# Row tails, router rows and the last attention denominators moved between engines in a two-layer mixture-of-experts backbone

## The chip, the cores and the metric

The kernel runs on one core of one Trainium2 chip. The metric is the device time of one execution in microseconds (us). The names of the engines are those of the profile: PE (matmuls), PEld (its weight loads), DVE (vector), ACT (scalar), POOL (GpSimd) and SP, which here only issues transfers. Each engine takes its instructions in order from a queue of its own, and semaphores make one engine wait for another.

## The reference, cut to what matters

512 latent and 256 context tokens of width 1024 pass through two post-norm layers. Layer 0 mixes with attention (8 neighbourhood heads and 8 grouped-query heads), layer 1 with two recurrences (RWKV-7 and mLSTM). After each mixer stand the output weight, a layer norm, a router that picks 6 of 64 experts for each token, the experts, one shared expert and a second layer norm. Layer 1 keeps the latent tokens alone.

```python
x = layer_norm(DN_ALPHA * x + g1 * (m_lat @ mix_w_out[i]), ln_g[i, 0], ln_b[i, 0])
h_lat = x * (1.0 + sc2) + sh2
...
scores = jax.nn.sigmoid((xt @ router_w).astype(F32))
_, idx = lax.top_k(scores + router_b.astype(F32), TOP_K)
gates = jnp.take_along_axis(scores, idx, -1)
...
y = yb.reshape(n_rows, D) * row_gate[:, None]
return jax.ops.segment_sum(y, row_tok, num_segments=n_tok + 1)[:n_tok]
...
x = layer_norm(DN_ALPHA * x + g2 * y[:B * S].reshape(B, S, D), ln_g[i, 1], ln_b[i, 1])
```

## The kernel before, in words

Tokens lie in tiles of 128 rows: six in layer 0 (four latent, two context), four in layer 1. A scheduler that simulates a timeline sets the order on each engine's queue, so moving one line of code can move others; what it chose is read from the order rows below. Stages of the profiled execution, in us from the start of the span:

- 0 to 485: layer 0's attention. A head pair (a "row" of `mT`) is closed by `close_block`: the reciprocal of the sums (L614, `rs`), the eviction of the unnormalized output, then three steps on POOL's queue: a transfer of `rs` to DRAM (L617), two transfers back that spread it over 64 partitions each (L620), and a multiply (L622). The last row is row 3.
- 485 to 640: the output weight. `weights` loads it in blocks and splits each into two parts, `w_hi` on ACT (L409) and `w_lo` on DVE (L410); `mT` is split in the same way, row by row; three matmuls (L414 to L416) make one product. The load buffer `w` shares a tag, and so memory, with `h2`. Then for each tile `first_norm` (L1087 to L1091: two DVE passes make `h`, one ACT and two POOL passes make the row `x` that the second norm needs) and `route` (L951 to L979: logits, the six best, `mask`, ranks and gates).
- 640 to 660: `sort` makes the list of each expert's tokens: gates in three parts (L932 to L936), one-hot rows `oh` (L1179), list matmuls (L1184); instructions L1363 to L1383 count what overflows the planned units.
- 660 to 1352: the routed experts of layer 0 in 49 units: a gather (L1207), transposes (L1258, L1260, L1261), up (L1217 into `pb`), gate, down (L1217 into `pp`), eviction of `py` to `y` in halves (L1247 on ACT, L1248 on DVE), and a scatter that adds to `acc` in DRAM (L1249).
- 1352 to 1404: the second norm's rows: the sums come back (L1410), then for each tile add, times g2 (L1415, L1416, halves on DVE and POOL), the residual (L1417), statistics (L878 to L882) and ACT's L1419.
- 1404 to 2161: the recurrent layer; it sends small state tiles through DRAM by SP (L2178 and L2181).
- 2161 to 2254: output weight, router and sort of layer 1; to 2861 its 37 units; to 2923 its end: the last scatters, L1410 to L1419 for four tiles, the final gain and offset (L2417 and L2418: DVE takes 640 columns, POOL 384), and the store.

The functions that the diff touches, with their line numbers:

Of the kernel before, what the change touches and what calls it, by code (L numbers as in the profile page):

```python
# [12 lines left out]
F32 = mybir.dt.float32  # L13
# [3 lines left out]
AF = mybir.ActivationFunctionType  # L17
# [338 lines left out]
class Kern:  # L356
# [152 lines left out]
    def attention(self, mT):  # L509
# [100 lines left out]
        def close_block(po, sums, out):  # L610
# [4 lines left out]
            self.copy(out, po)  # L615
            d = self.dr.tile([2 * n, 128], F32, name="rsum", tag=f"rsum{n}", bufs=2)
# [7 lines left out]
        def outputs(g, b, pTs, v, cols, state, sums, row):  # L624
# [5 lines left out]
            if b == 3:  # L630
                close_block(state[g], sums[:, 0:4], mT[:, row, 0:NLAT])
            if b == 5:
                close_block(state[g], sums[:, 4:6], mT[:, row, NLAT:])
# [253 lines left out]
    def layer_tail(self, layer, mT, x_rows, finish, part=None, done=None):  # L887
# [7 lines left out]
        with ExitStack() as es:  # L895
# [34 lines left out]
            def gates(dst, src, rest):  # L930
# [5 lines left out]
                nc.vector.tensor_copy(dst[:, :, :, 5], rest)  # L936
# [86 lines left out]
            with ExitStack() as es2:  # L1023
# [5 lines left out]
                def weights(b, parts=None):  # L1029
# [52 lines left out]
                def first_norm(t):  # L1082
# [13 lines left out]
                if layer == 0:  # L1096
                    room = Room(ring.tile([128, 2048], F32, name="sw1"),
# [25 lines left out]
                sw += [third(i["shared_w"][layer, k], ring, f"sw{k}") for k in range(len(sw), 3)]  # L1123
# [11 lines left out]
            def sort():  # L1135
# [33 lines left out]
                gates(aux, pq[:, :, 1], gq)  # L1169
# [68 lines left out]
            def down(hT, parts, ws, idx):  # L1238
# [8 lines left out]
                nc.scalar.copy(y[:, 0:512], py[:, 0:512])  # L1247
                nc.vector.tensor_copy(y[:, 512:], py[:, 512:])  # L1248
# [4 lines left out]
            def columns_of(xg):  # L1253
# [3 lines left out]
                for k in range(KT):  # L1257
                    nc.tensor.transpose(p[:, k], xg[:, k * 128:(k + 1) * 128], self.k_ident[:n, :n])  # L1258
                out = wp.tile([128, KT, 128], F32, name="xT", tag="xT", bufs=2)[:, :, :n]
                nc.scalar.copy(out[:, 0:4], p[:, 0:4])  # L1260
                nc.vector.tensor_copy(out[:, 4:8], p[:, 4:8])  # L1261
# [94 lines left out]
            for _ in side:  # L1356
                pass
# [1082 lines left out]
```

## Time and profile before

| | us |
|---|---|
| median of 3 runs | 2927.14 (2916.27 to 2935.19) |
| the profiled execution | 2924.99 |
| its span, first to last instruction | 2923.0 |

| engine | busy us | share of the span |
|---|---|---|
| PE | 2418.9 | 83% |
| DVE | 1214.3 | 42% |
| POOL | 760.8 | 26% |
| ACT | 737.1 | 25% |

The granted TensorE clock is 0.898 of full speed over the span, and the transfers move 247 GB/s in the mean. The shares are averages over stages with different limits: what one stage waits for is read from that stage's own rows.

### The profile page before, as it was taken

What the parts mean: (1) busy time and instruction counts of PE and PEld (TensorE: products, weight loads), DVE (VectorE), ACT (ScalarE), POOL (GpSimd) and SP (SyncE); (2) the same over time, 40 slices, a digit from 0 to 9 for tenths busy, and PEclk for the clock granted to TensorE, in tenths of its full rate; (3) what the DMA queues carried; (4) which work ended last, traced back from release to release, by engine and by line L of the source; (5) the groups of instructions that cost most, each with busy time, mean ns of one, the idle gap of its engine ahead of it and who ended that gap; (6) DMA issues with size and microseconds to landing.
All of it is one profiled execution on the core that took longest, in us unless ns stands there. A gap on an engine that the chain in (4) does not pass through costs nothing. (4 is left out here: it accounts for less than half of the span.)

```text
span 2923.0 us, 45988 instructions
## 1 busy us (share of the span) xinstructions
PE 2418.9 (83%) x18007; PEld 1469.8 (50%) x18007; DVE 1214.3 (42%) x2595; ACT 737.1 (25%) x1605; POOL 760.8 (26%) x674
## 2 busy tenths in 40 slices
PE   7789895969989999994799778866866988979981
PEld 6658664854434444331578666756755333324330
DVE  5742544473212222213753577856566212111114
ACT  3442443231101111111554443413222101111102
POOL 0111011121112222214344354434622111111114
PEclk9899997879999999997899787879976999999995
DMA  8644445658999999996224445589635999999993
GB/s 315 213 127 124 111 132 99 236 199 313 377 343 327 359 332 347 378 343 197 86 71 111 132 126 153 145 238 299 241 129 214 383 378 354 358 393 353 353 378 115
DMA packets 254089, 722.31 MB, mean 247 GB/s; under 512 B 111096, under 2 KB 137464, under 8 KB 194736
## 3 DMA queue, kind: packets, MB, share of 16 engines
q1 hardware_dynamic: 216656, 631.86, 59.2%
q0 software_dynamic: 26560, 68.09, 9.3%
q10 hardware_dynamic: 10656, 19.40, 2.1%
q8 instruction: 143, 2.34, 0.4%
q14 instruction: 74, 0.61, 0.1%
HBM read 636.45 MB, written 107.33 MB: 254 GB/s over the span
## 5 line engine op out<-in xcount | busy, mean ns | idle before, releaser
L1217 PE MATMUL pb<-ew,xT 128*32 128x512 f32 (+2 forms) x3504 | 658.6, 605 | 24.4 <-DMA ew<-in_moe_w_dram 15.4
L1217 PEld LDWEIGHTS pb<-ew,xT 128*32 128x32 f32 (+2 forms) x3504 | 210.5, 127 | 397.3 <-issue 353.9
L1217 PE MATMUL pp<-ew,hT 128*32 128x512 f32 (+2 forms) x1752 | 327.2, 603 | 7.7 <-DMA ew<-in_moe_w_dram 5.2
L1432 DVE SCALAR_TENSOR_TENSOR hs<-s,gate,pb 128x256 f32<-128x256 f32 x86 | 41.3, 480 | 649.7 <-ACT s L1427 633.9
L1207 POOL DMA_INDIRECT xg<-rows,idx x86 | 88.8, 1032 | 649.4 <-PE pp L1258 276.0
L1427 ACT ACTIVATE s<-pb 128x256 f32<-128x256 f32 x96 | 36.1, 383 | 769.9 <-PE pb L1217 746.7
L1249 POOL DMA_INDIRECT acc<-ye,idx x86 | 137.0, 1593 | 323.9 <-DMA acc<-ye,idx 146.8
L1217 PEld LDWEIGHTS pp<-ew,hT 128*32 128x32 f32 (+2 forms) x1752 | 101.6, 126 | 189.1 <-issue 175.0
L414 PE MATMUL pp<-h_hi,w_hi 128*128 128x512 f32 (+1 forms) x432 | 162.5, 377 | 8.7 <-DVE mT L389 4.3
L415 PE MATMUL pp<-h_lo,w_hi 128*128 128x512 f32 (+1 forms) x432 | 159.7, 370 | 1.0 <-DVE h_lo L410 1.0
L416 PE MATMUL pp<-h_hi,w_lo 128*128 128x512 f32 (+1 forms) x432 | 159.7, 371 | 0.5 <-POOL w_lo L1570 0.5
L1570 POOL TENSOR_TENSOR w_lo<-w,w_hi 128x512 fp32r<-128x512 f32 x66 | 91.6, 1388 | 148.3 <-ACT w_hi L1569 127.9
L1258 PEld LDWEIGHTS pp<-consts,xg 128*128 128x128 f32 x688 | 79.5, 146 | 70.5 <-issue 47.4
L1258 PE MATMUL pp<-consts,xg 128*128 128x128 f32 x688 | 98.3, 288 | 14.4 <-DVE sh L1311 6.8
L1248 DVE COPY ye<-pp 128x512 f32<-128x512 f32 x86 | 59.1, 687 | 114.7 <-ACT ye L1247 109.6
L414 PE MATMUL pb<-w_hi,m_hi 128*128 128x256 f32 x256 | 77.9, 308 | 26.6 <-ACT w_hi L409 16.2
L414 PEld LDWEIGHTS pp<-h_hi,w_hi 128*128 128x128 f32 x432 | 86.9, 202 | 24.6 <-issue 6.8
L416 PEld LDWEIGHTS pp<-h_hi,w_lo 128*128 128x128 f32 x432 | 87.0, 202 | 16.4 <-issue 3.4
L440 PE MATMUL pb<-ada_w,cz 128*32 128x256 f32 x640 | 54.1, 456 | 49.6 <-DMA ada_w<-in_ada_w_dram 49.5
L1261 DVE COPY xT<-pp 128x512 f32<-128x512 f32 x86 | 59.4, 690 | 84.9 <-ACT xT L1260 84.9
L415 PEld LDWEIGHTS pp<-h_lo,w_hi 128*128 128x128 f32 x432 | 87.3, 202 | 14.1 <-issue 2.3
L1247 ACT COPY ye<-pp 128x512 f32<-128x512 f32 x86 | 50.4, 588 | 166.3 <-PE pp L1217 110.0
(515 smaller groups left out, 4737.5 us busy)
## 6 DMA issues: line engine op xcount, KB each, us to landing
ew<-in_moe_w_dram SPq DMA_DIRECT2D x384, 1024.0 KB
ada_w<-in_ada_w_dram SPq DMA_DIRECT2D x48, 1024.0 KB
w<-in_rec_w_dram ACTq DMA_DIRECT2D x66, 256.0 KB
steps<-dL SPq DMA_DIRECT2D x16, 1024.0 KB
acc<-zero SPq DMA_DIRECT2D x12, 1024.0 KB
ew<-acc SPq DMA_DIRECT2D x10, 1024.0 KB
w<-in_att_w_dram SPq DMA_DIRECT2D x18, 512.0 KB
cells<-dM SPq DMA_DIRECT2D x8, 1056.0 KB
```

The source lines that it names most:

```text
L414: mm(out, l_hi, r_hi, start=start, stop=False)
L415: mm(out, l_hi, r_lo, start=False, stop=False)
L416: mm(out, l_lo, r_hi, start=False, stop=stop)
L440: nc.tensor.matmul(p[32 * g:32 * g + 32], self.cz[:, 4 * a + g, 30 - 2 * i:62 - 2 * i], w[:, 4 * a + g, :], start=i + a == 0, stop=i + 1 = ...
L1207: nc.gpsimd.indirect_dma_start(out=xg, out_offset=None, in_=self.rows[layer], in_offset=bass.IndirectOffsetOnAxis(ap=idx, axis=0), bounds_ ...
L1217: nc.tensor.matmul(out[s], x[:, s], ws[m], start=start, stop=stop, tile_position=(0, s.start))
L1247: nc.scalar.copy(y[:, 0:512], py[:, 0:512])
L1248: nc.vector.tensor_copy(y[:, 512:], py[:, 512:])
L1249: nc.gpsimd.indirect_dma_start(out=self.acc[layer], out_offset=bass.IndirectOffsetOnAxis(ap=idx, axis=0), in_=y, in_offset=None, bounds_ch ...
L1258: nc.tensor.transpose(p[:, k], xg[:, k * 128:(k + 1) * 128], self.k_ident[:n, :n])
L1261: nc.vector.tensor_copy(out[:, 4:8], p[:, 4:8])
L1570: nc.gpsimd.tensor_tensor(lo, w, hi.bitcast(F32), op=OP.subtract)
```

## The change

1. `close_block` has an argument `at_once`, true for row 3: the reciprocals stand on diagonals (DVE, new L623), a matmul with ones spreads them (PE, L624), and DVE multiplies (L626). The other rows keep POOL's way.
2. `first = loaded_part()`: the first load buffer of the output weight is allocated ahead of the other tiles.
3. Layer 0's first shared weight is loaded after the loop over tiles.
4. `first_norm`: ACT's pass and POOL's two become two DVE passes, new L1105 and L1106.
5. The overflow count is issued after the last `columns_of`; the gather for unit 2 waits for the sort and the first transposes.
6. In layer 1 the eviction multiplies by g2 (one DVE instruction of 1024 columns), and g2's row is loaded ahead of the first gathers.
7. `finish`, with the final gain's and offset's loads, is called ahead of the last `close`.
8. The second norm's rows are whole DVE instructions; in the last layer two of them take the place of L1419 and of the four half passes.

```diff
-        def close_block(po, sums, out):
+        def close_block(po, sums, out, at_once):
...
+            if at_once:
+                pr = self.bank((128, n * 128))
+                diag = ap.tile([128, 512], F32, name="r", tag="r", bufs=1)
+                for b in range(n):
+                    for s in range(2):
+                        d = diag[:, 256 * (b % 2) + 128 * s:][:, :128]
+                        nc.vector.tensor_scalar(d, self.k_ident, rs[:, s * n + b:s * n + b + 1], None, op0=OP.mult)
+                        nc.tensor.matmul(pr[s * 64:s * 64 + 64, b * 128:(b + 1) * 128], self.k_ones[:, 0:64], d,
+                                         start=True, stop=True, tile_position=(0, 64 * s))
+                nc.vector.tensor_tensor(out, out, pr, op=OP.mult)
+                return
...
-                close_block(state[g], sums[:, 0:4], mT[:, row, 0:NLAT])
+                close_block(state[g], sums[:, 0:4], mT[:, row, 0:NLAT], row == 3)
...
+                def loaded_part():
+                    return rp.tile([128, 4, 256], F32, name="w", tag="h2", bufs=2)
...
-                        w = rp.tile([128, 4, 256], F32, name="w", tag="h2", bufs=2)
+                        w = first if first is not None and k == 0 else loaded_part()
...
+                first = loaded_part()
...
-                w = [weights(0, w0)]
+                w = [weights(0, w0, first)]
...
-                    nc.scalar.activation(x, x, AF.Identity, bias=both, scale=over)
-                    nc.gpsimd.tensor_tensor(x, x, ra, op=OP.mult)
-                    nc.gpsimd.tensor_tensor(x, x, rbb, op=OP.add)
+                    nc.vector.scalar_tensor_tensor(x, x, less, ra, op0=OP.add, op1=OP.mult)
+                    nc.vector.scalar_tensor_tensor(x, x, over, rbb, op0=OP.mult, op1=OP.add)
...
-                sw = [third(i["shared_w"][layer, k], ring, f"sw{k}") for k in range(3 if layer else 1)]
+                sw = [third(i["shared_w"][layer, k], ring, f"sw{k}") for k in range(3 if layer else 0)]
...
+                if layer == 0:
+                    nc.sync.dma_start(sw0, i["shared_w"][layer, 0])
+                    sw = [sw0] + [third(i["shared_w"][layer, k], ring, f"sw{k}") for k in (1, 2)]
...
-                nc.scalar.copy(y[:, 0:512], py[:, 0:512])
-                nc.vector.tensor_copy(y[:, 512:], py[:, 512:])
+                if layer:
+                    nc.vector.tensor_tensor(y, py, g2[0], op=OP.mult)
+                else:
+                    nc.scalar.copy(y[:, 0:512], py[:, 0:512])
+                    nc.vector.tensor_copy(y[:, 512:], py[:, 512:])
...
+            if layer:
+                g2 = [self.row(wp, layer, "g20")]
...
-            sort()
+            sorted_ = sort()
             load()
-            xgs[2] = fetch(slot_of(2)[0])
             xT = columns_of(xgs.pop(0))
+            with tc.issue_after(columns_of.last.ins), tc.issue_after(sorted_.ins):
+                xgs[2] = fetch(slot_of(2)[0])
...
+            fresh = lambda: wp.tile([128, 2048], F32, name="ew", tag="ew", bufs=RING)
+            done = finish(fresh)
             close(len(units) - 1)
...
+            late = ExitStack()
+            late.enter_context(tc.issue_after(columns_of.done.ins))
...
-                for eng, c in zip((nc.vector, nc.gpsimd), half):
-                    eng.tensor_tensor(y[:, c], y[:, c], more[:, c], op=OP.add)
-                    eng.tensor_tensor(y[:, c], y[:, c], g2[st[t]][:, c], op=OP.mult)
+                nc.vector.tensor_tensor(y, y, more, op=OP.add)
+                if not layer:
+                    nc.vector.tensor_tensor(y, y, g2[st[t]], op=OP.mult)
                 nc.vector.scalar_tensor_tensor(x, y, 1.0, x, op0=OP.mult, op1=OP.add, accum_out=sums[:, t:t + 1])
-                less, over, both = self.spread(wp, x, sums[:, t:t + 1], y)
-                nc.scalar.activation(x, x, AF.Identity, bias=both, scale=over)
-                done(t, x)
+                done(t, x, *self.spread(wp, x, sums[:, t:t + 1], y))
...
-                for eng, c in ((nc.vector, slice(0, 640)), (nc.gpsimd, slice(640, D))):
-                    eng.tensor_tensor(x[:, c], x[:, c], gain[:, c], op=OP.mult)
-                    eng.tensor_tensor(x[:, c], x[:, c], offset[:, c], op=OP.add)
+                nc.vector.scalar_tensor_tensor(x, x, less, gain, op0=OP.add, op1=OP.mult)
+                nc.vector.scalar_tensor_tensor(x, x, over, offset, op0=OP.mult, op1=OP.add)
```

DVE's queue at the last heads and the split of `mT`, before (L614 is the reciprocal of the last sums, L389 copies out of PSUM):

```order
L614 RECIPROCAL rs<-sums_3889 128x2x2
L389 COPY pT<-pb 128x256 x2
L389 COPY mT<-pb 128x256
L1047 MEMSET sums 128x24
L410 TENSOR_TENSOR m_lo<-mT,m_hi 128x768 x7
L410 TENSOR_TENSOR w_lo<-w,w_hi 128x1024 x2
L943 CAST upper<-consts 128x128
```

and with the change:

```order
L615 RECIPROCAL rs<-sums_3889 128x2x2
L623 TENSOR_SCALAR r<-consts,rs 128x128
L389 COPY pT<-pb 128x256
L626 TENSOR_TENSOR mT<-mT,pb 128x512
L623 TENSOR_SCALAR r<-consts,rs 128x128 x4
L389 COPY mT<-pb 128x256
...
L626 TENSOR_TENSOR mT<-mT,pb 128x256
L410 TENSOR_TENSOR m_lo<-mT,m_hi 128x768
```

The multiply now stands on DVE right behind the eviction, and all eight `m_lo` stand ahead of both `w_lo`; before, seven stood there and the eighth behind POOL's multiply.

DVE's queue in layer 0's sort, before (L1363 to L1383 are the overflow count, L932 to L936 the gates):

```order
L1383 CAST blk<-ov 1x1
L932 CAST aux<-pp 128x384
L1179 TENSOR_TENSOR oh<-slot,rk 128x768
...
L1371 TENSOR_REDUCE oc<-ov 128x1
L933 TENSOR_TENSOR ye<-pp,aux 128x384
```

and with the change, where they are L944 to L948 and `oh` is L1197:

```order
L944 CAST aux<-pp 128x384
L945 TENSOR_TENSOR ye<-pp,aux 128x384
L946 CAST aux<-ye 128x384
L947 TENSOR_TENSOR ye<-ye,aux 128x384
L948 CAST aux<-ye 128x384
L1197 TENSOR_TENSOR oh<-slot,rk 128x768
```

The count has left this place, and the gates stand together ahead of the one-hots. On PE the first eight transposes (L1258, now L1279) stand ahead of the list matmuls instead of behind them.

SP's queue in the recurrent layer, before (state tiles to DRAM and back):

```order
L2030 DMA dL_11595<-Arb_15989 128x2x256
L2178 DMA dT_13241<-Tb_15976 64x16x16 x4
L2030 DMA dL_11595<-TT_15860 128x2x256
L1884 DMA cells_16424<-in_mlstm_order_dram 128x256
L2181 DMA T0_13238<-dT_13241 64x8x64 x8
```

and with the change, though no line of that layer is edited:

```order
L2054 DMA dL_11595<-Arb_15989 128x2x256
L2202 DMA dT_13241<-Tb_15976 64x16x16 x2
L1925 DMA cells_16423<-dR_11600 128x1024
L2205 DMA T0_13238<-dT_13241 64x8x64
L2202 DMA dT_13241<-Tb_15976 64x16x16
L2205 DMA T0_13238<-dT_13241 64x8x64
```

Writes and reads of the same state now alternate here; before, four writes stood together ahead of eight reads.

## Rows read from the trace of the kernel before

**Rows 1.** Windows: stretch, its us, PE busy (instructions), granted clock, DMA share, GB/s.
```profile
485.00:516.00 31.00, 9.84 (x42) 0.56 0.94 197
562.00:640.00 78.00, 57.90 (x440) 0.82 0.41 153
2254.00:2400.00 146.00, 129.88 (x939) 0.96 1.00 391
```

**Rows 2.** Timeline of PE: start, us, engine, line, operation, [idle before <-releaser].
```profile
495.70 1.01 PE L414 MATMUL pb<-w_hi,m_hi 128*128 128x256 f32 x3 [10.75 <-ACT w_hi L409]
...
511.80 0.58 PE L414 MATMUL pb<-w_hi,m_hi 128*128 128x256 f32 x1 [10.21 <-ACT m_hi L409]
```

**Rows 3.** Timeline of POOL and of SP, the same stretch.
```profile
510.17 0.71 POOL L622 TENSOR_TENSOR mT<-mT,r 128x256 f32<-128x256 f32 x1 [3.03 <-DMA r<-rsum]
484.99 0.80 SPq L1033 DMA_DIRECT2D w<-in_w_out_dram  x2
```

**Rows 4.** Timeline of DVE, the same stretch.
```profile
486.21 5.29 DVE L410 TENSOR_TENSOR m_lo<-mT,m_hi 128x768 fp32r<-128x768 f32 x6
491.44 1.23 DVE L410 TENSOR_TENSOR w_lo<-w,w_hi 128x1024 fp32r<-128x1024 f32 x1
...
497.23 0.22 DVE L946 TENSOR_SCALAR slot<-consts 128x128 bf16<-128x128 f32 x1
```

**Rows 5.** Groups of DVE by form, 560 to 660: form, count, busy us, mean ns, idle.
```profile
L969 DVE CAST mask<-m 128x128 bf16<-128x128 f32 x6 | 7.8, 1306 | 0.2
...
L1088 DVE SCALAR_TENSOR_TENSOR h<-h,rstd,B 128x1024 f32<-128x1024 f32 x6 | 7.7, 1278 | 0.0
L968 DVE TENSOR_TENSOR m<-rep,bi 128x64 f32<-128x64 f32 x6 | 6.4, 1074 | 0.2
```

**Rows 6.** Timelines of DVE and POOL in one router tile.
```profile
588.61 0.23 DVE L962 TENSOR_TENSOR bi<-sc,bias 128x64 f32<-128x64 f32 x1
...
594.60 2.38 DVE L969 CAST mask<-m 128x128 bf16<-128x128 f32 x1
...
594.56 2.34 POOL L1091 TENSOR_TENSOR x<-x,rb 128x1024 f32<-128x1024 f32 x1
```

**Rows 7.** Timeline of PE in the two sorts, layer 0 then layer 1.
```profile
658.65 0.58 PE L1184 MATMUL pb<-aux,oh 128*128 128x6 bf16 x30 [7.84 <-DVE aux L936]
...
2250.37 0.38 PE L1184 MATMUL pb<-aux,oh 128*32 128x6 bf16 x32 [5.90 <-DVE oc L1374]
2250.68 3.27 PE L1258 MATMUL pp<-consts,xg 128*128 128x128 f32 x16
```

**Rows 8.** What DVE's half eviction L1248 waited for, 2254 to 2861: us, times.
```profile
  ACT ye L1247: 39.1, 13
```

**Rows 9.** Groups of DVE by form, 1360 to 1405, second norm of layer 0.
```profile
L1417 DVE SCALAR_TENSOR_TENSOR x<-ew,x 128x1024 f32<-128x1024 f32 x6 | 10.1, 1688 | 1.5 <-POOL ew L1416 1.2
L1415 DVE TENSOR_TENSOR ew<-ew 128x512 f32<-128x512 f32 x6 | 7.2, 1200 | 15.6 <-DMA ew<-acc 15.6
L1416 DVE TENSOR_TENSOR ew<-ew,g 128x512 f32<-128x512 f32 x6 | 7.0, 1161 | 0.1
L882 DVE TENSOR_TENSOR rstd<-rstd 128x1 f32<-128x1 f32 x6 | 3.0, 506 | 0.1
```

**Rows 10.** Timelines of SP and DVE: sums fetched and first used, layer 0 then 1.
```profile
1363.89 3.30 SPq L1410 DMA_DIRECT2D ew<-acc  x6
...
1368.99 0.69 DVE L1415 TENSOR_TENSOR ew<-ew 128x512 f32<-128x512 f32 x1 [15.58 <-DMA ew<-acc]
...
2878.18 2.37 SPq L1410 DMA_DIRECT2D ew<-acc  x4
...
2885.72 0.69 DVE L1415 TENSOR_TENSOR ew<-ew 128x512 f32<-128x512 f32 x1 [18.73 <-DMA ew<-acc]
```

**Rows 11.** Timeline of POOL, its last row, at the end.
```profile
2916.85 1.45 POOL L2418 TENSOR_TENSOR x<-x,ew 128x384 f32<-128x384 f32 x1
```

**Rows 12.** Waits of PE in the recurrent layer: us in total, times, longest.
```profile
PE pb L394 <- DMA T<-dT: 13.1, 2, 8.4
```

More of the change, by code (lines that the diff above doesn't have):

```diff
@@ L630, in outputs @@
             if b == 3:
-                close_block(state[g], sums[:, 0:4], mT[:, row, 0:NLAT])
+                close_block(state[g], sums[:, 0:4], mT[:, row, 0:NLAT], row == 3)
             if b == 5:
-                close_block(state[g], sums[:, 4:6], mT[:, row, NLAT:])
+                close_block(state[g], sums[:, 4:6], mT[:, row, NLAT:], row == 3)
         def run_blocks(items, first, second, third, lag):
@@ L1027, in layer_tail, with weights @@
                 w_parts = lambda: [rp.tile([128, mk, 256], F32R, name=v, tag=v, bufs=wb) for v in ("w_hi", "w_lo")]
-                def weights(b, parts=None):
+                def loaded_part():
+                    return rp.tile([128, 4, 256], F32, name="w", tag="h2", bufs=2)
+                def weights(b, parts=None, first=None):
                     hi, lo = parts or w_parts()
                     for k in range(0, mk, 4):
-                        w = rp.tile([128, 4, 256], F32, name="w", tag="h2", bufs=2)
+                        w = first if first is not None and k == 0 else loaded_part()
                         self.loads = nc.sync.dma_start(w, i["w_out"][layer, b, :, k:k + 4])
@@ L1122, in layer_tail @@
                     pass
-                sw += [third(i["shared_w"][layer, k], ring, f"sw{k}") for k in range(len(sw), 3)]
+                if layer == 0:
+                    nc.sync.dma_start(sw0, i["shared_w"][layer, 0])
+                    sw = [sw0] + [third(i["shared_w"][layer, k], ring, f"sw{k}") for k in (1, 2)]
                 route(rp, turn[-1], hs.pop(turn[-1]))
@@ L1168, in sort @@
                 nc.scalar.copy(rk, pq[:, :, 0])
-                gates(aux, pq[:, :, 1], gq)
+                return gates(aux, pq[:, :, 1], gq)
             def slots(members, at):
@@ L1257, in columns_of @@
                 for k in range(KT):
-                    nc.tensor.transpose(p[:, k], xg[:, k * 128:(k + 1) * 128], self.k_ident[:n, :n])
+                    columns_of.last = nc.tensor.transpose(p[:, k], xg[:, k * 128:(k + 1) * 128], self.k_ident[:n, :n])
                 out = wp.tile([128, KT, 128], F32, name="xT", tag="xT", bufs=2)[:, :, :n]
                 nc.scalar.copy(out[:, 0:4], p[:, 0:4])
-                nc.vector.tensor_copy(out[:, 4:8], p[:, 4:8])
+                columns_of.done = nc.vector.tensor_copy(out[:, 4:8], p[:, 4:8])
                 return out
@@ L1349, in layer_tail @@
                     slot_of(n + LISTS)
-                if n == 6:
+                if n == 6 and not layer:
                     with tc.issue_after(self.loads.ins):
@@ L1383, in layer_tail @@
             nc.vector.tensor_copy(blk[:, 128:129], cum[0:1, NE - 1:NE])
+            late.close()
             n_more = nc.values_load(blk[0:1, 128:129], min_val=0, max_val=127)
@@ L1400, in layer_tail @@
                 down(gated(up(xT, all_of, [w[0:2]]), gate[:, 0:1]), all_of, [w[2]], idx[:, 1])
-            fresh = lambda: wp.tile([128, 2048], F32, name="ew", tag="ew", bufs=RING)
-            done = finish(fresh)
             sums = wp.tile([128, nt], F32, name="sums")
-            half = slice(0, 512), slice(512, D)
             ys = {}
@@ L2388, in keep, with rows @@
         def keep(room):
-            def rows(t, x):
+            def rows(t, x, less, over, both):
+                nc.scalar.activation(x, x, AF.Identity, bias=both, scale=over)
                 if t < 4:
@@ L2413, in store, with rows @@
             gain, offset = (k.row(None, 1, v, out=w[:, n * D:n * D + D]) for n, v in enumerate(("fg", "fb")))
-            def rows(t, x):
-                for eng, c in ((nc.vector, slice(0, 640)), (nc.gpsimd, slice(640, D))):
-                    eng.tensor_tensor(x[:, c], x[:, c], gain[:, c], op=OP.mult)
-                    eng.tensor_tensor(x[:, c], x[:, c], offset[:, c], op=OP.add)
+            def rows(t, x, less, over, both):
+                nc.vector.scalar_tensor_tensor(x, x, less, gain, op0=OP.add, op1=OP.mult)
+                nc.vector.scalar_tensor_tensor(x, x, over, offset, op0=OP.mult, op1=OP.add)
                 nc.sync.dma_start(out[0, t * 128:(t + 1) * 128], x)
```

3 lines of the change are left out of this document (2 added, 1 removed).

## The prediction

> **What bounds the kernel now.** I read the windows by stage first, then PE's timeline for its idle stretches, then, for what ended each, the timelines and the groups by form of the engine named. PE is busy 83% of the span, so a saving counts only where PE, or the end of the program, waits for it. The reader should see four kinds of stretch. Between the attention and the output weight PE works 9.84 of 31 us [rows 1]: it waits 10.75 us for ACT's `w_hi` and then 10.21 us for ACT's last `m_hi` [rows 2]. In layer 0's router PE is busy 57.9 of 78 us [rows 1]. The experts of layer 1 are bound by transfers: DMA share 1.00 [rows 1]. In the second norms PE has nothing to do, and DVE and POOL set the length.
>
> **The change, part by part.** The sum is made against the profiled execution, 2924.99 us; the median of the three runs, 2927.14, is 2.15 above it.
>
> *Attention to output weight (edits 1 to 3).* Before, the last denominators go through DRAM; the last multiply starts at 510.17, having waited 3.03 us for the spread rows [rows 3]. Then ACT casts, and PE starts at 511.80 [rows 2]. The two weight loads are issued only at 484.99 [rows 3], when the last attention matmuls have freed the memory of their buffer. With the change both loads can be issued during the attention, and eight diagonals (price: the 128x128 tensor-scalar, 0.22 [rows 4], so 1.8 us) lie on a DVE that then waits for PE. I follow DVE's new queue: the last multiply ends at about 486; small casts and fills some 3.5 us; eight `m_lo` at 5.29/6 = 0.88 each, 7.1; two `w_lo` at 1.23, 2.5 [rows 4]. That ends at about 499. In the trace of before both `w_lo` and the eighth `m_lo` were done, and PE ran without gaps, from about 512 on. PE has about 5 us of the first products to do in either case and can do them while DVE still splits. 512 - 499 is 13; I take **12** because ACT now casts eight `m_hi` ahead of the first `w_hi`. Bounds: 8 (only the second wait goes) and 14. The first shared weight hides behind the tiles: it is first used with the experts, after 640; without that cover its 1 MB costs 2.7 us, at the 391 GB/s of [rows 1].
>
> *Router rows (edit 4).* What goes is not POOL's time but what it does to DVE. A 64-column tensor-tensor takes 0.23 us on DVE alone; the mask's cast takes 2.38 when it starts within POOL's 2.34 us multiply-add [rows 6]. Over six tiles the mean is 1.306 for that cast and 1.074 for L968 [rows 5]; against 0.23 that is 1.08 + 0.84 = 1.9 us a tile, and three more small forms lose about 1.1 between them, so about 3.1 in all. Added are two passes of 1.28 (L1088's mean [rows 5]), 2.56, in front of the same mask. Net 0.5 a tile: **3** for six tiles in layer 0, 2 for four in layer 1. Bounds: 0 (the first of the two new passes also waits for ACT's square) and 9 in layer 0, if the idle stretches of the matmuls close.
>
> *Sorts (edit 5).* The list matmuls waited 7.84 us in layer 0 and 5.90 us in layer 1, there for `oc` of the overflow count [rows 7]. The count leaves, worth about 1 us of instructions between the gates (estimate from the order: eight instructions of the 64-column kind, partly behind ACT); and eight of the 16 transposes that follow in 3.27 us [rows 7] move into the wait, 1.6. I take **2.5** for each, between 1 and 5. The gather for unit 2 now waits for the sort; it is needed two units later (692 us for 49 units, so 28 us). The count itself ends up in DVE's idle time between the last units.
>
> *Layer 1 in transfers.* Its router and sort give 2 + 2.5; but the stage behind is bound by loads, which start with the router's end and not with the sort's. I count **3.5** (0 to 5). Edit 6 costs nothing there: DVE's half eviction already waited for ACT's (39.1 us in 13 cases [rows 8]), so one instruction ends about when two in a row did. g2's row is the same 0.5 MB, moved.
>
> The Trainium skill speaks against that edit: PSUM — Partial Sum Buffer, "Specifications (TRN2)", says that ScalarE and VectorE read PSUM in parallel at full bandwidth when they are on different banks. By it the halves cost 0.69 us together and one DVE instruction about 0.5 more, 37 times 18 us; the trace disagrees, for the halves ran one behind the other.
>
> *Second norm of layer 0 (edit 8).* DVE's rows for six tiles sum to 10.1 + 7.2 + 7.0 + 3.0 = 27.3 us [rows 9]. New: two whole tensor-tensors at 1.23, one pass at 1.28, 0.15 for L882: 3.9 a tile, 23.3. With the wait of 1.2 for POOL [rows 9] gone it is 5; DVE's queue also carries the reciprocal's wait for ACT, so I take **4** (2 to 6).
>
> *The end (edits 7 and 8).* In layer 0 DVE starts 5.1 us after the first issue of L1410, in layer 1 7.5 us after [rows 10]. The two rows ahead of it, 1 MB, are now loaded earlier, and SP's 0.86 us for them too: first sum at 2877.3 + 5.1 = 2882.4 instead of 2885.7. A tile then costs DVE 1.23 + 3 x 1.28 + 0.4 = 5.5 us, four tiles 22, and about 2 us of waits for ACT's squares at the first and last tile: 2906.4. Before, POOL's last row ended at 2918.3 [rows 11]. The store behind it stays. That is **12** (7 to 14).
>
> Sum: 12 + 3 + 2.5 + 3.5 + 4 + 12 = 37, so 2924.99 - 37 = **2888 us**. All lower bounds together are 18 (2907), all upper ones 53 (2872).
>
> **The rivals.**
>
> *The recurrent layer's new order takes it back.* No line of it is edited, but its queues are (SP's rows with `dT`). PE waits there 8.4 us at most for such a read [rows 12]. Writes and reads now alternate, so a read that waits for its write to land holds SP's next write. Against: many of these reads are not waited for (2 waits in all, 13.1 us). Two more waits make 2905, a chance of 0.17. **The slower side** is the same mechanism repeated: above five such waits (37 / 8.4 = 4.4) the kernel is slower than before, and with eight, 8 x 8.4 = 67, it takes 2955. Chance 0.06.
>
> *DVE becomes the bound.* If the slow small forms wait for something other than POOL, nothing comes back for the 2.56 us a tile: instead of 3 and 2 gained, 15 and 10 lost in front of `route`, part of it hidden behind PE's matmuls of the next tile; half of it on the path gives 2888 + 5 + 12 = 2905. For it: DVE has more to do in every stage touched. Against: start and end of the cast and of POOL's row coincide [rows 6]. Chance 0.10.
>
> *The clock comes back too.* From 485 to 516 the granted clock is 0.56, in the router 0.82 [rows 1], that is 1.2 GHz for part of the time, behind the idle stretches. If these close, up to 0.18 of 78 us is run at 2.4 GHz where it was 1.2, and half of that was bound by PE: 7 us more, and by likeness as much in layer 1's router, so 2874. Against: the stretches there are cut, not closed. Chance 0.07. The Trainium skill (TensorE: Matmul & The Clock Gate, "What's actually happening") states the rule behind it, that activity releases the throttle; the trace agrees in the clock of those stretches.
>
> *The change doesn't do what it says.* If the buffers moved ahead meet another tile's memory, the loads still wait for the attention and only the second wait goes: 2892, inside the forecast's range.
>
> **How the numbers follow.** Forecast 0.60 (2872 to 2907), clock 0.07, order with two more waits 0.17, DVE 0.10, slower 0.06. The range is 2868 to 2913: below it lies a share of the clock's case, above it the slower case and the tails of the two at 2905. A measurement of this kernel tells about 1% from no change: 2898 and 2956. Under 2898: five sixths of the forecast, the clock, a sixth of the two at 2905, 0.50 + 0.07 + 0.05 = 0.62. Slower by over 1%: half of the slower case, 0.03. Within 1%: 0.35.
>
> **What would show it.** PE's 10.75 and 10.21 us gone, with the matmuls of the output weight dense from about 499. The mask's cast near 0.25 in every tile. PE's waits in the sorts at 5 and 4 us. The first sum at the end about 5 us after its issue, DVE's 1024-column passes at 1.2 to 1.3, and the last one about 12 us ahead of POOL's 2918.3, less what came before. The recurrent layer as long as before, 757 us, within 8. It is wrong if that layer lengthens by more, or if whole-row passes cost 2 us with POOL silent.

## The result and the profile after

| | before | changed |
|---|---|---|
| median of 4 runs, us | 2921.7 (2915.5 to 2935.19) | 2875.44 (2870.79 to 2889.01) |
| the profiled execution, us | 2924.99 | 2889.01 |
| its span, us | 2923.0 | 2887.2 |
| granted clock | 0.898 | 0.900 |
| busy DVE / POOL / ACT, us | 1214.3 / 760.8 / 737.1 | 1214.1 / 661.6 / 705.5 |

The changed kernel takes 0.983 of the time before (95% interval 0.980 to 0.986), 1.7% less; the forecast was 2888 in 2868 to 2913. The medians lie 46 us apart, the two spans 35.8: the profiled execution of the changed kernel is the slowest of its four. What follows goes by the spans, and by stages within them. DVE's busy time is the same although it took over POOL's passes: it no longer stands still inside its own instructions.

The table gives each stage's length from the first start (or last end) of a named instruction to the next, in the traces of before, of the change, and of the changed kernel run once more ("again").

| stage | before | after | again |
|---|---|---|---|
| to the last attention matmul (L607) | 485.0 | 493.5 | 494.1 |
| to layer 0's first router transposes (L903) | 80.7 | 67.6 | 66.3 |
| to the sort (L1158) | 81.2 | 71.3 | 70.0 |
| to the first up matmul (L1217) | 15.8 | 12.8 | 12.8 |
| to the fetch of the sums (L1410) | 701.2 | 697.4 | 697.8 |
| to the recurrent layer's first projection (L414) | 42.8 | 37.9 | 38.0 |
| to its last projection | 491.2 | 489.4 | 484.8 |
| to layer 1's output weight | 267.7 | 280.5 | 280.7 |
| to layer 1's first router transposes | 23.8 | 25.2 | 25.2 |
| to the sort | 51.9 | 46.9 | 46.9 |
| to the first up matmul | 12.4 | 10.8 | 10.1 |
| to the last down matmul | 607.4 | 608.5 | 608.7 |
| to the end | 61.9 | 45.4 | 45.8 |

Most stages that an edit touches became shorter. Three did not: the attention is 8.6 us longer, of which some 3 come with edit 1 (below), the units of layer 1 are 1.1 longer and the stretch ahead of layer 1's router 1.4. The recurrent layer became longer by 10.9 (its two parts together) without an edit.

The timeline of PE behind the attention, which answers to [rows 2] (L624 spreads the denominators):

```profile
493.29 0.93 PE L624 MATMUL pb<-r,consts 128*64 128x128 f32 x8
500.62 1.01 PE L414 MATMUL pb<-w_hi,m_hi 128*128 128x256 f32 x3 [6.41 <-ACT w_hi L409]
...
505.83 0.58 PE L415 MATMUL pb<-w_lo,m_hi 128*128 128x256 f32 x1 [1.74 <-DVE w_lo L410]
```

and DVE's, which answers to [rows 4]:

```profile
493.64 0.42 DVE L389 COPY mT<-pb 128x256 f32<-128x256 f32 x1
...
494.26 0.42 DVE L626 TENSOR_TENSOR mT<-mT,pb 128x256 f32<-128x256 f32 x1
...
498.20 5.31 DVE L410 TENSOR_TENSOR m_lo<-mT,m_hi 128x768 fp32r<-128x768 f32 x6
503.41 2.37 DVE L410 TENSOR_TENSOR w_lo<-w,w_hi 128x1024 fp32r<-128x1024 f32 x2
```

The last multiply ends 0.6 us after the eviction (L389) and 1.2 us behind the last attention matmul, where POOL's ended 25.9 us behind it. Dense matmuls begin 12.3 us behind the last attention matmul (505.83 - 493.52); before it was 26.8. DVE's `m_lo` and `w_lo`, one behind the other, set that moment.

The spreading costs PE time inside the attention. `ada_w` are weights that PE multiplies beside the attention (L440). PE's last wait for one of their loads there ends as follows, before and after:

```profile
460.56 1.94 PE L440 MATMUL pb<-ada_w,cz 128*32 128x256 f32 x16 [5.59 <-DMA ada_w<-in_ada_w_dram]
```
```profile
466.44 1.94 PE L440 MATMUL pb<-ada_w,cz 128*32 128x256 f32 x16 [5.24 <-DMA ada_w<-in_ada_w_dram]
```

From there to the last attention matmul it is 24.4 us before and 27.1 after, with 19 of L624's 24 matmuls in between. Over all traces it is 23.1 to 24.4 us in the three without edits 1 and 2 (before, before_again, dram_last) and 25.5 to 27.4 in the ten with them. So some 3 us of the attention's delay are the price of edit 1.

DVE's groups by form in layer 0's router, 560 to 633, which answer to [rows 5] (L981 is the mask's cast, L980 its comparison, L1105 and L1106 the new passes):

```profile
L1106 DVE SCALAR_TENSOR_TENSOR x<-x,rstd,rb 128x1024 f32<-128x1024 f32 x6 | 7.7, 1278 | 0.0
...
L981 DVE CAST mask<-m 128x128 bf16<-128x128 f32 x6 | 1.4, 227 | 0.2
L980 DVE TENSOR_TENSOR m<-rep,bi 128x64 f32<-128x64 f32 x6 | 1.4, 226 | 0.2
```

The cast's mean fell from 1306 to 227 ns, the comparison's from 1074 to 226. What PE waited for in the router (total us, times, longest), before and after:

```profile
PE pb L974 <- DVE mask L969: 7.0, 4, 3.0
```
```profile
PE pb L986 <- DVE mask L981: 1.6, 2, 1.3
```

PE in the sort of layer 0 and of layer 1, after, for [rows 7]:

```profile
638.85 1.94 PE L1279 MATMUL pp<-consts,xg 128*128 128x128 f32 x8 [2.50 <-DMA xg<-rows,idx]
642.25 0.32 PE L1202 MATMUL pb<-aux,oh 128*128 128x6 bf16 x6 [1.46 <-DVE oh L1197]
...
2230.68 1.94 PE L1279 MATMUL pp<-consts,xg 128*128 128x128 f32 x8 [5.13 <-DMA xg<-rows,idx]
```

In layer 0 the wait is shorter (2.50 and 1.46 us instead of 7.84), in layer 1 only a little (5.13 instead of 5.90). The longest wait has a new owner: the gather that feeds the first transposes, no longer the gates or the count.

The second norm of layer 0, DVE by form, for [rows 9], and the end of the program on SP and DVE, for [rows 10, 11]:

```profile
L1443 DVE SCALAR_TENSOR_TENSOR x<-ew,x 128x1024 f32<-128x1024 f32 x6 | 7.3, 1221 | 0.0
L1442 DVE TENSOR_TENSOR ew<-ew,g 128x1024 f32<-128x1024 f32 x6 | 7.3, 1220 | 0.1
L1440 DVE TENSOR_TENSOR ew<-ew 128x1024 f32<-128x1024 f32 x6 | 7.3, 1216 | 15.0 <-DMA ew<-acc 15.0
```
```profile
2857.79 2.19 SPq L1436 DMA_DIRECT2D ew<-acc  x4
...
2862.91 1.23 DVE L1440 TENSOR_TENSOR ew<-ew 128x1024 f32<-128x1024 f32 x1 [15.48 <-DMA ew<-acc]
...
2867.05 1.28 DVE L2441 SCALAR_TENSOR_TENSOR x<-x,rstd,ew 128x1024 f32<-128x1024 f32 x1 [0.35 <-ACT ew L891]
...
2880.78 1.28 DVE L2441 SCALAR_TENSOR_TENSOR x<-x,rstd,ew 128x1024 f32<-128x1024 f32 x1 [0.37 <-ACT ew L891]
...
2882.25 1.28 DVE L2442 SCALAR_TENSOR_TENSOR x<-x,rstd,ew 128x1024 f32<-128x1024 f32 x1
```

The residual pass takes 1221 ns in the mean, 1688 before. The first sum is used 5.1 us after its issue, and DVE is done at 2883.5; it waits for ACT's squares twice, 0.7 us in all.

### The profile page after: what moved, and what is told of

The parts are those of the page before. It is cut to its first block, busy times and chain, and to the rows that moved or that the text cites. A ratio compares the mean times of both kernels' runs of the same rounds, so it can differ in the third digit from the quotient of the medians.

```text
span 2887.2 us, 45906 instructions
## 1 busy us (share of the span) xinstructions
PE 2426.5 (84%) x18031; PEld 1477.0 (51%) x18031; DVE 1214.1 (42%) x2625; ACT 705.5 (24%) x1556; POOL 661.6 (23%) x618
## 5 line engine op out<-in xcount | busy, mean ns | idle before, releaser
L1235 PE MATMUL pp<-ew,hT 128*32 128x512 f32 (+2 forms) x1752 | 330.6, 607 | 13.1 <-DMA ew<-in_moe_w_dram 6.0
L414 PE MATMUL pp<-h_hi,w_hi 128*128 128x512 f32 (+1 forms) x432 | 161.3, 375 | 4.8 <-DVE mT L389 4.3
L1279 PEld LDWEIGHTS pp<-consts,xg 128*128 128x128 f32 x688 | 79.9, 147 | 77.0 <-issue 55.7
L1279 PE MATMUL pp<-consts,xg 128*128 128x128 f32 x688 | 99.1, 290 | 20.8 <-DMA xg<-rows,idx 7.6
L440 PE MATMUL pb<-ada_w,cz 128*32 128x256 f32 x640 | 56.1, 471 | 52.6 <-DMA ada_w<-in_ada_w_dram 52.6
L414 PEld LDWEIGHTS pp<-h_hi,w_hi 128*128 128x128 f32 x432 | 86.0, 200 | 20.5 <-DVE mT L389 4.4
L414 PE MATMUL pb<-w_hi,m_hi 128*128 128x256 f32 x256 | 76.8, 303 | 11.6 <-ACT w_hi L409 11.6
L1281 ACT COPY xT<-pp 128x512 f32<-128x512 f32 x86 | 50.3, 585 | 147.7 <-PE pp L1279 146.5
L598 PE MATMUL pb<-consts,P 128*128 128x128 f32 x384 | 70.6, 301 | 9.9 <-ACT P L854 5.3
```

What stands on the lines that cost most here:

```text
L414: mm(out, l_hi, r_hi, start=start, stop=False)
L440: nc.tensor.matmul(p[32 * g:32 * g + 32], self.cz[:, 4 * a + g, 30 - 2 * i:62 - 2 * i], w[:, 4 * a + g, :], start=i + a == 0, stop=i + 1 = ...
L598: nc.tensor.transpose(t[:, c - c0, :], p[:, c * 128:(c + 1) * 128], self.k_ident)
L1235: nc.tensor.matmul(out[s], x[:, s], ws[m], start=start, stop=stop, tile_position=(0, s.start))
L1279: columns_of.last = nc.tensor.transpose(p[:, k], xg[:, k * 128:(k + 1) * 128], self.k_ident[:n, :n])
```

## The experiments

Eleven kernels ran; each is the changed kernel with one edit, unless said otherwise. Edits 1 and 2 were undone together, and edit 3 by none of them. Ratios are to the kernel before on the same chip, with 95% intervals.

| kernel | ratio | span of its profile |
|---|---|---|
| again | 0.981 (0.979 to 0.983) | 2881.3 |
| dram_last | 0.988 (0.986 to 0.990) | 2900.0 |
| pool_tails | 0.986 (0.984 to 0.988) | 2880.7 |
| pool_busy | 0.992 (0.990 to 0.995) | 2921.4 |
| split_rows | 0.985 (0.982 to 0.987) | 2887.6 |
| late_rows | 0.985 (0.983 to 0.988) | 2880.9 |
| halves | 0.986 (0.983 to 0.988) | 2897.7 |
| count_early | 0.984 (0.982 to 0.986) | 2897.8 |
| order_back | 0.983 (0.980 to 0.986) | 2873.5 |
| setup_late | 0.981 (0.978 to 0.983) | 2873.7 |
| before_again | 1.001 (0.999 to 1.003) | 2928.2 |

Single executions of one kernel lie up to 27 us apart, so effects of 3 to 6 us are read from the stage that an edit touches, not from a span. The whole-run ratios of the undone edits agree in sign, but don't give their sizes. Against the ratio of "again", 0.981, they are larger than the stages show: some 21 us against 13 for dram_last, 15 against 9 for halves, 13 against 4 for late_rows. Against the 0.983 of the first runs the same three are 13, 7 and 6 us. The two ratios of one and the same kernel lie 8 us apart, so the difference isn't explained.

**again.** No edit.

> The changed kernel once more. Two things in its first trace have no edit behind them: the attention ends 8.6 us later than before, and the recurrent layer from its first projection to the output weight takes 769.9 us instead of 759.0. Theory (order): the recurrent layer's length belongs to the order of its queues, so it comes out at 768 to 772 again, while the attention's delay, which are waits for ada_w loads under an unchanged order, moves by several us. Rival (chance of the one execution): the recurrent layer comes out within 3 us of 759. Ratio to before 0.980 to 0.986 by both.

The recurrent layer took 765.5 us, its second part 280.7 (280.5 in the first trace), its first part 484.8 (489.4). That is short of the theory's 768 and beyond the rival's 762. The attention ended at 494.1, 0.6 us from the first trace. The second part repeats to 0.2 us in these two; four later traces in the same order have 273.6 to 279.2, so chance moves it too.

**dram_last.** Edits 1 and 2 undone.

```diff
-                close_block(state[g], sums[:, 0:4], mT[:, row, 0:NLAT], row == 3)
+                close_block(state[g], sums[:, 0:4], mT[:, row, 0:NLAT], False)
...
-                first = loaded_part()
...
-                w = [weights(0, w0, first)]
+                w = [weights(0, w0)]
```

> The changed kernel with the last denominators through DRAM again and the first load buffer not allocated ahead. Theory (two waits gone): the two idle stretches of 10.75 and 10.21 us come back, PE is dense from 26 to 28 us after the last attention matmul instead of 12, and the kernel takes 10 to 14 us more than the changed one. Rival (DVE's split sets the pace anyway): dense from 16 to 20 us after, 4 to 7 us more.

PE's timeline behind its last attention matmul at 490.7:

```profile
501.64 1.01 PE L414 MATMUL pb<-w_hi,m_hi 128*128 128x256 f32 x3 [10.98 <-ACT w_hi L409]
...
516.99 0.58 PE L414 MATMUL pb<-w_hi,m_hi 128*128 128x256 f32 x1 [9.46 <-ACT m_hi L409]
```

Both waits are back, and dense work starts 26.3 us behind the attention. To the first router transposes it is 80.7 us again, 13.1 more than in the changed kernel. Expected and found. What each of the two edits gives alone no run shows. Its layer 0 router takes 73.8 us, 2.5 and 3.8 more than in the changed kernel: as in the kernel before, 64 matmuls of L440 (those with `ada_w`) stand in it, and 48 where edits 1 and 2 are in.

**pool_tails.** Edit 4 undone.

```diff
-                    nc.vector.scalar_tensor_tensor(x, x, less, ra, op0=OP.add, op1=OP.mult)
-                    nc.vector.scalar_tensor_tensor(x, x, over, rbb, op0=OP.mult, op1=OP.add)
+                    nc.scalar.activation(x, x, AF.Identity, bias=both, scale=over)
+                    nc.gpsimd.tensor_tensor(x, x, ra, op=OP.mult)
+                    nc.gpsimd.tensor_tensor(x, x, rbb, op=OP.add)
```

> The changed kernel with first_norm's row tail back on ACT and POOL. Theory (POOL's passes hold up DVE's small instructions): the mask's cast is again 1.3 us in the mean of layer 0 instead of about 0.25, layer 0's stretch from the first router transposes to the sort is 8 to 11 us longer than in the changed kernel, layer 1's 4 to 6; the kernel takes 10 to 16 us more. Rival (the gain of the router came from elsewhere, the earlier weights or the closed idle stretches): the cast is slow again but the stretch grows by 3 us or less, as the prediction's net of 0.5 us a tile has it.

The cast's mean is 1302 ns. Layer 0's router takes 79.7 us (71.3 and 70.0 with the edit), layer 1's 52.0 (46.9). The edit is worth 8 to 10 and 5 us; its rival, 3 or less, is out. The windows of layer 0's router (columns as in [rows 1], with weight loads, DVE, ACT and POOL behind PE), first of pool_tails, then of the changed kernel:

```profile
556.00:637.00 81.00, 58.77 (x442) 52.26 (x442) 57.90 (x146) 33.01 (x58) 31.35 (x14) 0.76 0.44 166
```
```profile
561.00:633.00 72.00, 54.64 (x441) 49.00 (x442) 50.11 (x157) 26.80 (x52) 1.55 (x2) 0.80 0.49 180
```

Cut exactly at the stage's ends, the same 438 matmuls keep PE busy for 57.8 us in pool_tails and for 54.0 in the changed kernel; by the traces' clock records 24.0 and 16.5 us of that are at 1.2 GHz. PE's waits for the mask are 7.1 and 1.6 us. So nearly 4 of the 8 to 10 us are matmuls that run at the higher clock, and the rest are waits that went.

Its span equals that of "again" because of other stages: the recurrent layer 762.0 in a third order, layer 1's units 603.2, the end 41.2.

**pool_busy.** POOL works besides, for nobody; the extra tile is not part of the result.

```diff
+                    idle = rp.tile([128, 896], F32, name="idle")
+                    nc.gpsimd.tensor_tensor(idle, x[:, :896], ra[:, :896], op=OP.mult)
+                    nc.gpsimd.tensor_tensor(idle, idle, rbb[:, :896], op=OP.add)
```

> The changed kernel with POOL doing two multiply-add passes of 896 columns a tile besides, into a tile that nobody reads: DVE's instructions and their order stay. Theory (POOL's passes hold up DVE): DVE's 64 and 128 column forms that start within a POOL pass take 1.5 to 2.4 us, and layer 0's stretch from the first router transposes to the sort grows by 6 to 12 us. Rival (the forms were slow for another reason, their place in the queue): they stay at 0.2 to 0.3 us, and the stretch grows by under 2.

DVE's and POOL's timelines in one tile, 590 to 612:

```profile
595.32 2.08 DVE L980 TENSOR_TENSOR m<-rep,bi 128x64 f32<-128x64 f32 x1
597.44 2.12 DVE L981 CAST mask<-m 128x128 bf16<-128x128 f32 x1
599.48 0.21 DVE L988 SCALAR_TENSOR_TENSOR cat<-sc,m 128x64 f32<-128x64 f32 x1
```
```profile
595.23 2.09 POOL L1108 TENSOR_TENSOR idle<-x,ra 128x896 f32<-128x896 f32 x1 [15.75 <-DVE x L1106]
597.40 2.07 POOL L1109 TENSOR_TENSOR idle<-idle,rb 128x896 f32<-128x896 f32 x1
```

DVE's rows stand in the same order as in the changed kernel, where the same two forms take 0.23 us. Here each ends with the POOL pass in which it began: one pass costs one DVE instruction the whole length of the pass. PE's waits in the router:

```profile
PE pb L986 <- DVE mask L981: 14.9, 6, 3.7
```

Layer 0's router is 86.7 us long, 15.4 more, layer 1's 57.4, 10.5 more: more than expected, in the direction that only this theory has. Part of it is clock: PE is busy for 61.25 us at 0.73 in the window from 564 to 652, against 54.64 at 0.80 above. That it costs more than the old tail because DVE has its two passes as well is likely, but no run separates it.

**split_rows.** Edit 8 undone (g2 stays in layer 1's eviction).

```diff
-                nc.vector.tensor_tensor(y, y, more, op=OP.add)
+                    for eng, c in zip((nc.vector, nc.gpsimd), half):
+                        eng.tensor_tensor(y[:, c], y[:, c], more[:, c], op=OP.add)
...
-                nc.vector.scalar_tensor_tensor(x, x, less, gain, op0=OP.add, op1=OP.mult)
-                nc.vector.scalar_tensor_tensor(x, x, over, offset, op0=OP.mult, op1=OP.add)
+                nc.scalar.activation(x, x, AF.Identity, bias=both, scale=over)
+                for eng, c in ((nc.vector, slice(0, 640)), (nc.gpsimd, slice(640, D))):
+                    eng.tensor_tensor(x[:, c], x[:, c], gain[:, c], op=OP.mult)
+                    eng.tensor_tensor(x[:, c], x[:, c], offset[:, c], op=OP.add)
```

> The changed kernel with the second norm's rows halved again between DVE and POOL, in the last layer also the final gain and offset with ACT's pass (edit 8 undone; g2 stays in the eviction). Theory (POOL's halves hold up DVE and are slow themselves): the residual pass takes 2.1 to 2.3 us again beside POOL instead of 1.2 to 1.3, layer 0's stretch from the first fetch of the sums to the recurrent layer's first projection is 4 to 6 us longer than the changed kernel's 37.9, the end from the fetch to the last instruction 8 to 11 us longer than 29.4. Rival (the earlier loads of gain and offset, edit 7, gave most of the end): the end is 3 us longer or less.

DVE's residual pass by form in layer 0's second norm:

```profile
L1448 DVE SCALAR_TENSOR_TENSOR x<-ew,x 128x1024 f32<-128x1024 f32 x6 | 10.1, 1688 | 1.5 <-POOL ew L1447 1.2
```

Three of the six passes took 2.1 to 2.3 us, the others 1.2. From the fetch to the first projection it is 43.0 us, 5.1 more, as expected. The end from the fetch is 34.9, 5.5 more, less than the 8 to 11 expected: there all four residual passes took 1.2 us, where in the kernel before, with g2's halves on POOL, two of four took 2.1 and 2.3.

**late_rows.** Edit 7 undone.

```diff
-            fresh = lambda: wp.tile([128, 2048], F32, name="ew", tag="ew", bufs=RING)
-            done = finish(fresh)
             close(len(units) - 1)
...
+            fresh = lambda: wp.tile([128, 2048], F32, name="ew", tag="ew", bufs=RING)
+            done = finish(fresh)
             sums = wp.tile([128, nt], F32, name="sums")
```

> The changed kernel with the final gain's and offset's loads behind the last units again (edit 7 undone). Theory (SP's two issues and 1 MB ahead of the sums): the first sum is used 7.5 us after its issue instead of about 5, SP issues 0.9 us later, and the end from the last down matmul is 3 to 4 us longer. Rival (the rows' tails gave all of it): within 1 us of the changed kernel's end.

SP's and DVE's timelines at its end:

```profile
2848.88 2.41 SPq L1436 DMA_DIRECT2D ew<-acc  x4
...
2856.61 1.23 DVE L1440 TENSOR_TENSOR ew<-ew 128x1024 f32<-128x1024 f32 x1 [19.08 <-DMA ew<-acc]
```

The first sum is used 7.7 us after its issue, and the end takes 49.4 us from the last down matmul, 4.0 more. Expected and found.

**halves.** Edit 6 undone.

```diff
-                if layer:
-                    nc.vector.tensor_tensor(y, py, g2[0], op=OP.mult)
-                else:
-                    nc.scalar.copy(y[:, 0:512], py[:, 0:512])
-                    nc.vector.tensor_copy(y[:, 512:], py[:, 512:])
+                nc.scalar.copy(y[:, 0:512], py[:, 0:512])
+                nc.vector.tensor_copy(y[:, 512:], py[:, 512:])
```

> The changed kernel with layer 1's eviction in halves and g2 in the second norm (edit 6 undone). Theory (nothing in the transfer-bound units, but one more DVE pass of 1.23 us a tile at the end): the units' stretch from first up to last down within 3 us of the changed kernel's 608.5, the end 3 to 5 us longer. Rival (two engines in parallel evict sooner): the units' stretch 10 to 18 us shorter.

The units take 612.5 us (608.5 and 608.7 with the edit), 1 us more than the theory allowed, and the end 50.5, 5.1 more. Two engines don't evict sooner here: in all 37 pairs DVE's half began only after ACT's had ended, by 0.03 us or more, and so it was in the kernel before. Of 36 pairs DVE waited in 14, for 57.2 us in all; ACT's half takes 0.6, so most of that is what ACT itself waited for, scatters of earlier tiles above all. One whole DVE eviction took 1.20 to 1.23 us in the changed kernel, two halves in a row 1.3.

**count_early.** Edit 5 undone.

```diff
-            with tc.issue_after(columns_of.last.ins), tc.issue_after(sorted_.ins):
-                xgs[2] = fetch(slot_of(2)[0])
...
-            late.enter_context(tc.issue_after(columns_of.done.ins))
```

> The changed kernel with the overflow count and the third gather where they were (edit 5 undone). Theory (count between the gates, transposes behind the lists): from the sort to the first up matmul 15 to 16 us in layer 0 instead of 12.8, and about 12.4 in layer 1 instead of 10.8; the kernel takes 3 to 5 us more. Rival (the sort waits for its one-hots and gathers anyway): under 1 us in each.

The sort takes 15.8 us in layer 0 (12.8 with the edit) and 11.9 in layer 1 (10.8 and 10.1). Three us and 1 to 2, as expected. Its attention ended at 511.6, on which no edit bears: that makes most of its span.

**order_back.** Tiny ACT copies that shift the scheduler's simulated time.

```diff
+                if not layer and t == 3:
+                    for _ in range(20):
+                        nc.scalar.copy(y[:, 0:8], more[:, 0:8])
```

> The changed kernel with 20 copies of 8 columns on ACT behind the last row of layer 0's second norm; they move the simulated timeline by a few us, and the scheduler then orders the recurrent layer nearly as in the kernel before (95 rows of PE's queue differ from it, instead of 1203). Theory (the scheduler's order takes back time): from the first projection to the output weight 757 to 762 us, its second part (from the last projection on) 267 to 270 instead of 274 to 281; the copies cost 2 to 4 us in front, so the kernel is 0 to 6 us faster than the changed one. Rival (length by chance of the execution): second part 274 or more.

The second part took 269.4 us, both parts 761.7; the copies cost 3.0 in front. As theory had it. The windows of that part (columns as in [rows 1], with weight loads, DVE, ACT and POOL behind PE), first of the changed kernel, then of order_back and split_rows:

```profile
1870.00:2150.00 280.00, 197.40 (x2748) 171.26 (x2746) 171.18 (x399) 63.79 (x145) 126.66 (x130) 0.79 0.70 222
```
```profile
1869.00:2139.00 270.00, 192.73 (x2750) 167.31 (x2749) 167.62 (x395) 66.05 (x152) 125.58 (x130) 0.81 0.72 234
```
```profile
1877.00:2145.00 268.00, 191.56 (x2749) 165.76 (x2747) 168.17 (x393) 65.62 (x150) 125.03 (x130) 0.81 0.74 235
```

The same work, about 2750 matmuls, takes 10 to 12 us more in the changed order, about half of it as busy time of PE at a lower clock (197.40 us at 0.79 against 192.73 and 191.56 at 0.81). Of all eleven kernels and the two first traces, the five in the old order or nearly so (before, before_again, dram_last, split_rows, order_back) took 267.7 to 269.4 us there, the six in the changed order (after, again, pool_busy, late_rows, halves, count_early) 273.6 to 280.7 (pool_tails and setup_late have orders of their own: 262.0 and 276.4). The part ahead of it went the other way, 489.9 to 492.3 against 482.2 to 489.6. Both together: 757.8 to 761.7 against 757.7 to 769.9, in the means 760.0 and 764.8. The changed order costs about 5 us in the mean, not the 10.9 of one pair of traces; the two ranges touch, so the figure is rough. Whole runs don't tell order_back from the changed kernel.

**setup_late.** Setup casts held back; `split_done` is the second `w_lo`.

```diff
-                with tc.issue_after(self.loads.ins):
+                with tc.issue_after(self.loads.ins), tc.issue_after(split_done.ins):
```

> The changed kernel with the router's small setup casts (DVE, seven instructions of 0.2 to 0.5 us) held behind the second w_lo. Theory (DVE's split sets when PE runs densely behind the attention): the wait for w_lo ends 1.3 to 2 us sooner after the last attention matmul, and the first router transposes come as much sooner after it than 67.6 us. Rival (ACT's casts or PE set it): under 0.5 us.

PE's timeline, its last attention matmul ending at 493.2:

```profile
504.21 0.58 PE L415 MATMUL pb<-w_lo,m_hi 128*128 128x256 f32 x1 [0.44 <-DVE w_lo L410]
```

The wait ends 11.0 us behind the attention instead of the 12.3 of all nine other traces with edits 1 and 2, and the router's transposes come 65.4 us behind it (67.6 and 66.3): DVE's split sets the pace. Whole runs show no gain that can be told from the changed kernel.

**before_again.** The kernel before, unedited.

> The kernel before once more. Theory (the attention's end moves between executions with its ada_w loads, under one order): it ends anywhere from 485 to 500 us instead of at 485.0 again; the recurrent layer takes 756 to 762 from first projection to output weight, the two sorts and the end within 1 us of the first trace. Rival (the changed kernel's attention is slower by its own doing): the end at 484 to 486 again.

The attention ended at 489.0, the recurrent layer took 760.7, the sorts 15.5 and 12.6, the end 62.2. The stages that were compared repeat; the attention's end doesn't. Over all traces it lies between 485.0 and 511.6, with all five queues in one order up to 480, but for edit 2's two loads at the end of SP's. What moves most is PE's waits for `ada_w` loads, 49.5 us in all before, 56.6 in before_again and 69.5 in count_early. The attention ended at 485 and 489 before, and at 489 to 512 in the others. Some 3 us of that are L624's matmuls (above). The last wait for an `ada_w` load ended at 460.6 to 466.7 in the three traces without edits 1 and 2, and at 462.7 to 472.1 in the others (484.6 in count_early). That the change also delays these loads by a few us isn't excluded; why they come later is open.

## Why the prediction was right

The forecast was a sum of six terms. Against the stages (after and again):

| step | forecast gain | measured gain |
|---|---|---|
| attention to output weight | 12 (8 to 14) | 13.1 and 14.4 |
| router rows, layer 0 | 3 (0 to 9) | 9.9 and 11.2 |
| sort, layer 0 | 2.5 (1 to 5) | 3.0 and 3.0 |
| layer 1's router and sort | 4.5, counted as 3.5 | 6.6 and 7.3 |
| layer 0's second norm | 4 (2 to 6) | 4.9 and 4.8 |
| the end | 12 (7 to 14) | 16.5 and 16.1 |
| recurrent layer | 0 | lost 10.9 and 6.6 |
| attention | 0 | lost 8.6 and 9.1, some 3 by edit 1 |

The forecast held by its range (2875.44 in 2868 to 2913), and most mechanisms were as told. The sizes were not: three terms lie above their upper bounds in both traces and a fourth in one of them. By the whole runs the gain is 46 us between the medians, and 57 in "again", so the sum of 37 is too small. That it comes near the 35.8 of the profiled pair is luck: that execution is the slowest of its four, and two losses that the sum had at nothing cancel what the terms had too small.

- **Attention to output weight.** The path was as followed: multiply, `m_lo`, `w_lo`, dense work. dram_last brings back the 13 us, and setup_late shows that DVE's split is the last in the chain. The term put PE's spreading matmuls at nothing; they cost some 3 us ahead of the attention's end, so that the net gain is 10 to 11.
- **Router rows: mechanism right, size too small.** The stalls come back with POOL's passes (pool_tails) and grow with added ones (pool_busy). The term failed at "Net 0.5 a tile". DVE's busy time in the stretch fell from 56.4 us of 82 to 50.1 of 72 although eleven passes of 1.28 came into it, so about 20 us of stalls went, 3.4 a tile rather than 3.1, net 0.8. The rest was PE's. Stalls stood in front of the mask that PE waited for, 7.0 us, and after the change 1.6, while no other of PE's waits there grew by more than 0.7 us for the added passes: all of them together fell from 23.2 us to 17.2. With the shorter waits the same matmuls ran at a higher clock (pool_tails). And 2 to 4 us of the 9.9 and 11.2 belong to edits 1 and 2, which move a block of matmuls out of the stretch (dram_last). An estimate in DVE's busy time alone missed on whose path each microsecond lay. The Trainium skill, SBUF — State Buffer, "Who interferes with whom", states that VectorE and GpSimd share a pair of ports under an exclusive lock, held for the whole instruction; the 2.08 and 2.12 us beside POOL's 2.09 and 2.07 agree.
- **Sorts.** Right in size in layer 0; in layer 1 it gave 1.6 and 2.3 us instead of 2.5. The new wait is for the gather (2.50 and 5.13 us), which the prediction didn't name.
- **Layer 1 in transfers.** No later bound took the router's and sort's gain back that can be told from chance: the units took 608.5 and 608.7 us against 607.4 and 604.1 (before_again), and 603 to 614 over all traces. Whether the discount of 1 us was needed can't be read from these. The Trainium skill's rule of two engines reading PSUM side by side (PSUM — Partial Sum Buffer, "Specifications (TRN2)") wasn't put to use here: in halves, as before, DVE's half began after ACT's had ended in all 37 pairs. What holds it back isn't shown.
- **The end.** Its parts by undoing: g2 in the eviction 5.1, loads earlier 4.0, whole rows 5.5. A tile took 5.2 us, less than the 5.5 priced, because passes of 1.28 start 1.2 apart, and the waits for ACT's squares were 0.7 us and not 2.
- **Rivals.** The recurrent layer's new order did take time back, about 5 us in the mean of eleven traces. It was not through the reads of `dT` that the prediction named: PE waited for them 13.1 us before and 4.7 in the changed kernel. The longest new waits there, 11.7 and 10.8 us, are for DVE's `mT` and `BK`. So that rival's place was wrong and its sign right. The prediction named a layer that is over 8 us longer as a sign that it is wrong: the first trace shows that sign (10.9), "again" doesn't (6.6). DVE as the bound is out: its busy time didn't grow. The clock came back in part: the router's stretch has 0.78 before and 0.80 after, and pool_tails shows nearly 4 us of matmul time by it, where the rival counted 7. In the recurrent layer's second part it went the other way, 190.55 us of busy PE at 0.83 before and 197.40 at 0.79 after.

Three us less in layer 0's units stand in every variant's trace (686, in setup_late 683, against 689) and weren't traced to an edit; edit 3 is the only one that no run undid.

## What to carry to other kernels

Price POOL's elementwise passes by what they do to DVE: each can hold one small DVE instruction for its whole length, and if PE waits for that instruction the pass is on the path though POOL is never the last releaser by name. Read such a stall from the same form's durations, a mean of 1306 ns here where the same form alone takes 227, and then ask which engine waits for it. The price can include PE's clock: here the same 438 matmuls took 57.8 us with the stalls and 54.0 without. When a scheduler orders the queues by simulated time, count a few us of gain or loss in stages that nobody edited, and read effects of this size from stages, not from one pair of spans.

## What the runs showed of the hardware

- Not only passes with two inputs: DVE's cast of one 128x64 tile (128x128 out) also waited for a POOL pass to end, 2.12 us instead of 0.23 (pool_busy).
- Of two POOL passes in a row each held one DVE instruction (pool_busy): L980 ended at 597.40, 0.08 us after the first pass, and L981 was held from 597.44 by the pass that began at 597.40.
- 1024-column DVE passes with two tensor inputs took 1.22 us (tensor-tensor), 1.28 with a per-row scalar besides, and started 1.2 us apart.
